# One encoder layer in fp32: operands at one place in 256 bytes, and the first head's turns and scores beside the last projection

## The chip, the cores and the metric

The kernel runs on one core of one Trainium2 chip. The metric is the device time in microseconds (us) of one execution. The engines are PE (TensorE, the matmuls), PEld (its weight loads), DVE (VectorE), ACT (ScalarE), POOL (GpSimd) and SP (SyncE). SP computes nothing here: it issues DMA transfers, one after the other, in the order of its list, and SPq is its queue.

## What is computed

One layer of a hybrid encoder runs on two sequences of 512 tokens with 1024 channels each, in fp32. Eight heads of 64 channels do a dilated window attention, 512 channels go through a gated long convolution (by FFT), both are normalized and projected together, and an MLP with squared ReLU follows.

```python
def encoder_layer(x, ...):
    xn = rmsnorm(x, mix_norm)
    proj = xn @ w_in                       # q, k, v (512 columns each), u (3 x 512)
    q = rope(rmsnorm_f32(q, q_norm)); k = rope(rmsnorm_f32(k, k_norm))
    attn = dilated_attention(q, k, v).reshape(B, S, ATTN_WIDTH)
    hy = hyena_mixer(u, hy_conv_w, hy_conv_b, hy_skip, spectra)
    mixed = jnp.concatenate([rmsnorm_f32(attn, attn_out_norm), rmsnorm_f32(hy, hy_out_norm)], axis=-1)
    h = x + mixed @ w_out
    hn = rmsnorm(h, ffn_norm)
    ff = jnp.square(jax.nn.relu(hn @ w_up))
    return h + ff @ w_down
```

The window branches of the attention are one masked softmax here: the mask and the weights of the branches lie in one table of biases (128 rows, 896 columns, `c_bias`), from which each 128 x 512 block of scores reads a shifted window.

## The kernel before

Every fp32 product is made of three matmuls on numbers split into a high and a low part (`mm3`, L85 to L92: high by high, high by low, low by high). A split costs one ACT copy, which rounds to the high part, and one DVE subtraction.

The stages, in the order of time: norm of the inputs; the projection to u (`proj_u`, psum tiles `psu`); the projection to q, k and v (`proj_qkv`, L539, `psq`, six calls, each of one of q, k, v and half of its columns, the last one Q21: v, second half); beside these the two streams of the convolution (HA and HB in the code, `psf` and `psi` are the matmuls of their FFTs, `z` is their running product, `hy_d` its copy in DRAM); then the attention with the hyena half of the output projection beside it; the attention's half of the output projection; the MLP's up projection (`pu`, `pn` from `hn`) and its down projection (`chi`, `clo`).

The attention goes by pairs of heads. `attn_load` (L778) brings q and k of a pair (tiles `qin`, two transfers each) and v. `stage_t(j, k)` (L795) turns q or k of pair j on PE with four 128 x 128 transposes into one psum bank `psk`, and splits the bank for both heads into tiles `qk`; of k it copies the high and the low part to the other 64 partitions by DMA (L812, `qk<-qk` in the trace, on SP). `stage_a(n, t)` (L815) makes a 128 x 512 block of scores of head n with two matmuls (`pss`), adds the bias and takes the maximum on DVE (`pe<-pss,bias`) and the exponential on ACT. `stage_b` (L834) turns four blocks of exponentials (`psp`) and splits the turned block into `ph`, `pl`; `stage_v` (L845) multiplies with v (`pv`). `attention` (L898) loads two pairs, turns k and q of pair 0, makes five blocks of scores ahead, and then goes through the heads.

`w_out_hyena` (L950) runs beside the attention: it loads the weights (`wur`, L758, four transfers of 512 KB), reads the convolution's result back (`hyr`, L958, two buffers), turns it (`psm`, L768) and multiplies (`psw`). It begins when both streams HA and HB are done.

`interleave` (L499) sets in which order the streams give their instructions to a scheduler, by costs that each step names; the scheduler then sets the order on every engine, and each engine runs its own list in that order. So a PE instruction that waits for a DMA holds up all PE work behind it, and a transfer in SP's list whose data isn't there holds up all transfers behind it.

Tiles lie in pools that open and close: `la` and `lw` (left side) hold the projection's inputs and weights, the raw weights `wraw`, the outputs `y`/`qo`/`vo` and the small tiles with the tag `ut`; `start_attention` (L707) closes both, opens `rm` and `lb` in their place and loads the bias table (L716). `lb` holds everything of the attention, its eight buffers of exponentials `pe` among them. The pool `cp`, opened first, stays to the end and lies below all others on the left side. In the MLP, `hn[k, half]` is in two pools: half 0 on the right side, half 1 (`hnB`) on the left.

Worked out from the allocation of the program: before, the large tiles on the left side start at byte 128 within 256 (the split inputs `xh`, `xl` and weights `whi`, `wlo` of the projections, `qk`, `bias`, `v`, `mh`, `ml`, half 1 of `hn`, among others) or at byte 32 (`pe`, `ph`, `pl`); those on the right side start at byte 224 (`chl`, `yh`, `yl`, half 0 of `hn`, `chi`, `clo`).

Of the kernel before, what the change touches and what calls it, by code (L numbers as in the profile page):

```python
# [8 lines left out]
F32 = mybir.dt.float32  # L9
F32R = mybir.dt.float32r  # L10
# [15 lines left out]
WB = 6  # L26
# [24 lines left out]
def r32(t):  # L51
    return t.bitcast(F32R)
# [3 lines left out]
def hybrid_encoder_kernel(ctx: ExitStack, tc: tile.TileContext, i: dict, outs, dbg=None):  # L56
# [62 lines left out]
    ssh = cp.tile([128, 8, 4], F32, name="ssh")  # L119
    ones = cp.tile([128, 1], F32, name="ones")  # L120
    nc.vector.memset(ones, 1.0)
    rsc = cp.tile([128, 4, 8], F32, name="rsc")
    ssd = cp.tile([128, 2, 8], F32, name="ssd")
# [8 lines left out]


    la, la_close = open_pool("la")
    lw, lw_close = open_pool("lw")
# [35 lines left out]
    def norm_x(s):  # L171
        for t in range(4):
            x = xs[s, t]
            c = slice(4 * s + t, 4 * s + t + 1)
            junk = [lw.tile([128, 512], F32, name="junk", tag=("y", "ut")[k], bufs=2) for k in range(2)]
# [20 lines left out]
    def load_w(src, first=False):  # L196

        out = []
        for k in range(src.shape[1]):
            hi = lw.tile([128, 512], F32R, name="whi", tag="whi", bufs=WB)  # L200
            lo = lw.tile([128, 512], F32R, name="wlo", tag="wlo", bufs=WB)
            raw = (re_.tile([128, 512], F32, name="wraw", tag="t", bufs=TB) if first and k > 1 else
                   lw.tile([128, 512], F32, name="wraw", tag="wraw", bufs=4))
            nc.sync.dma_start(raw, src[:, k])
            act(hi, raw)
            tt(nc.vector, lo, raw, f32(hi), ALU.subtract)
            out.append((hi, lo))
        return out
# [165 lines left out]
    def proj_u(q, w=None):  # L374
# [4 lines left out]
        def turn(s, a, y):  # L379
            pt = bank("pst", "tr", [128, 4, 128])  # L380
            for t in range(4):
                nc.tensor.transpose(pt[:, t], y[:, t * 128:(t + 1) * 128], ident)  # L382
            ut = lw.tile([128, 4, 128], F32, name="ut", tag="ut", bufs=2)
            act(ut, pt)
# [136 lines left out]
    def rope_tables():  # L521
        cs = lw.tile([128, 4, 2, 32], F32, name="cs", tag="y", bufs=2)
        nc.sync.dma_start(cs, i["c_rope"])
        g = lw.tile([128, 2, 64], F32, name="g", tag="ut", bufs=2)
# [4 lines left out]
        ng = lw.tile([128, 2, 64], F32, name="ng", tag="ut", bufs=2)  # L529
        nc.gpsimd.tensor_scalar(ng, g, -1.0, None, op0=ALU.mult)  # L530
# [8 lines left out]
    def proj_qkv(which, half):  # L539

        w = [(hi[:, c:c + 256], lo[:, c:c + 256]) for hi, lo in load_w(w_qkv[which, half]) for c in (0, 256)]
        for mp in range(4):
            s, t0 = divmod(2 * mp, 4)
# [16 lines left out]
            o = lw.tile([128, 2, 256], F32, name="qo", tag="y", bufs=2)  # L560
            sq = lw.tile([128, 2, 256], F32, name="sq", tag="ut", bufs=2)
            rr = lw.tile([128, 8], F32, name="rr", tag="rr", bufs=3)
# [19 lines left out]

    ab = lw.tile([128, 4, 4, 64], F32, name="ab")
    w0 = load_w(w_u[0], first=True)
# [193 lines left out]
    def attn_load(p, s):  # L778
        ins = []
        for src in (q_d, k_d):  # L780
            t = lb.tile([128, 4, 128], F32, name="qin", tag="qin", bufs=QIB)
            for m in range(2):
# [4 lines left out]
        nc.sync.dma_start(v2.rearrange("p t h d e -> p t (h d e)"),  # L787
                          v_d[s * S:(s + 1) * S, 2 * p:2 * p + 2].rearrange("(t p) h d e -> p t (h d e)", p=128))
        return ins[0], ins[1], r32(v2)


    PAIRS = [(s, 2 * g + p) for g in range(2) for s in range(NSEQ) for p in range(2)]
    split, ats, den_of, sta, exps, sqs = {}, {}, {}, {}, {}, {}

    def stage_t(j, k):  # L795


        ps = bank("psk", "tr")
        for t in range(4):
            lined(nc.tensor.transpose(ps[:, t * 128:(t + 1) * 128], split[j][k][:, t], ident))  # L800
        for g in range(2):
            a, b = slice(64 * g, 64 * g + 64), slice(64 - 64 * g, 128 - 64 * g)
            hi = lb.tile([128, 512], F32R, name="qk", tag="qk", bufs=QKB)
            act(hi[a], ps[a])
# [3 lines left out]
            else:  # L808
                lo = lb.tile([128, 512], F32R, name="qk", tag="qk", bufs=QKB)
                tt(nc.vector, lo[a], ps[a], f32(hi[a]), ALU.subtract)  # L810
# [4 lines left out]
    def stage_a(n, t):  # L815

        j, h = divmod(n, 2)
        if t == 0:
            if h == 0:
                den_of[j] = lb.tile([128, 4, 2], F32, name="den", tag="den", bufs=2)  # L820
            exps[n] = [lb.tile([128, 4], F32, name="mx", tag="mx", bufs=3)]
        den, mx = den_of[j], exps[n][0]
        ps = bank("pss", "ss")
        for e, kk in enumerate(sta[n, 1]):
            lined(nc.tensor.matmul(ps, lhsT=sta[n, 0][:, t * 128:(t + 1) * 128], rhs=kk, start=e == 0, stop=e == 1))  # L825
        e = lb.tile([128, 512], F32, name="pe", tag="pe", bufs=8)
        nc.vector.tensor_tensor_reduce(out=e, in0=ps, in1=bias[:, 384 - 128 * t:896 - 128 * t], scale=1.0, scalar=3e38,
                                       op0=ALU.add, op1=ALU.min, accum_out=mx[:, t:t + 1])
# [69 lines left out]
    def attention():  # L898
        load_pair(0)
        load_pair(1)  # L900
        for k in (1, 0):
            stage_t(0, k)
            yield 0.4, 0.6, 0
        ahead = [(n, t) for n in range(NI) for t in range(4)]

# [4 lines left out]

        for t in range(5):
            scores()
            yield 0.47, 1.0, 0
        stage_t(1, 1)
        yield 0.4, 0.6, 0


        for n in range(NI + 1):
# [6 lines left out]
            for t in range(4 if n < NI else 3):  # L925
# [11 lines left out]
                if t == (1, 3)[k] and j < len(PAIRS):  # L937
                    stage_t(j, k)
                    yield 0.4, 0.6, 0
                if scores():  # L940
                    yield 0.47, 1.0, 0
                if t and n < NI:
# [6 lines left out]
    def w_out_hyena():  # L949
# [4 lines left out]
        for s in range(NSEQ):  # L954
# [6 lines left out]
            for t in range(4):  # L961
# [17 lines left out]
        stream(("HA", ("r",), hyenas((0, 2)))),  # L979
        stream(("HB", ("r",), hyenas((1, 3)))),  # L980
        stream(*[(f"U{q}", (), proj_u(q, w0 if q == 0 else None)) for q in range(4)],
               *[(f"Q{w}{g}", (), proj_qkv(w, g)) for g in range(2) for w in range(3)],
               ("B", (), start_attention()), ("A", (), attention())),
        stream(("C", ("HA", "HB", "S"), w_out_hyena()), ("D", (), end_w_out_hyena()), ("E", ("A0",), w_out_first()),
# [109 lines left out]
    w_out_part(1, between)  # L1094
    rm_close.close()
    hnB, hnB_close = open_pool("hnB")
    hn_pool(hnB, 1)
# [383 lines left out]
```

## Time and profile before

| what | us |
|---|---|
| median of 3 runs (lowest, highest) | 1307.53 (1306.56, 1308.41) |
| the profiled execution, its own time | 1307.71 |
| its span, first to last instruction | 1305.9 |

| stretch, us from the span's start | what runs |
|---|---|
| 340 to 434 | q, k, v projections with the convolution streams beside them; the last projection ends near 431 |
| 434 to 481 | the end of stream HB, the first pairs of the attention, loads of the output projection |
| 481 to 640 | attention with the hyena half of the output projection beside it |
| 640 to 700 | attention's half of the output projection, norm |
| 700 to 985 | MLP up, 128 x 512 matmuls back to back |
| 1000 to 1290 | MLP down |

The page gives busy time by engine. A time between the starts of two matmuls is what one of them costs when PE is never idle, since a matmul's own duration overlaps with its successors. PEclk is the clock that was granted to PE, as a share of its full speed.

### The profile page before, as it was taken

Reading aid. Unit: us, or ns where it says so; the run is one execution under the profiler, and the core shown is the slowest. Engines: PE = TensorE matmul, PEld = TensorE weight load, DVE = VectorE, ACT = ScalarE, POOL = GpSimd, SP = SyncE. Lnnn points to the kernel's source line nnn. Section 1 sums busy time; section 2 is a strip of 40 time slices with the busy share of each in tenths; the row PEclk is TensorE's granted clock in tenths of the full one; section 3 lists DMA queues with packets and bytes.
Section 4 is the critical chain, followed back from the end, with each engine's and each line's share of the span. In section 5 each row is a group of like instructions: output and inputs, shape, how many; then the busy total and the mean of one; then the engine's idle time right before and its main releaser. Section 6 shows DMA issues by size and latency. Waiting matters only on the chain.

```text
span 1305.9 us, 18860 instructions
## 1 busy us (share of the span) xinstructions
PE 1258.5 (96%) x6733; PEld 1066.4 (82%) x6733; DVE 1013.9 (78%) x1584; ACT 650.5 (50%) x1430; POOL 175.6 (13%) x151
## 2 busy tenths in 40 slices
PE   6999999999999679999999999999999999999998
PEld 5788889999999568787777888888887888887887
DVE  6787668898997678978479877777757688578884
ACT  6444435664565485767456533343335654333350
POOL 2110002452343131124031000000000000001000
PEclk9999999999999889999999999999999999999999
DMA  7545433224411694535323544454347853473223
GB/s 244 182 138 178 148 108 101 92 90 143 138 66 66 185 269 157 153 99 185 118 92 113 173 162 142 145 161 138 129 156 279 290 160 115 161 257 93 88 70 121
DMA packets 137988, 192.82 MB, mean 148 GB/s; under 512 B 10332, under 2 KB 71684, under 8 KB 137893
## 3 DMA queue, kind: packets, MB, share of 16 engines
q1 hardware_dynamic: 136452, 185.06, 44.2%
q0 software_dynamic: 864, 4.46, 0.9%
q10 hardware_dynamic: 576, 2.10, 0.4%
q8 instruction: 53, 0.87, 0.3%
q14 instruction: 43, 0.34, 0.1%
HBM read 124.72 MB, written 62.65 MB: 143 GB/s over the span
## 4 chain that ended last, share of the span: by engine, by line
PE 79%; DVE 10%; DMA 5%; ACT 3%; issue 2%; SPq 1%; POOL 0%; DVEq 0%; ACTq 0%; POOLq 0%
PE pu L91 24%; PE pn L91 19%; PE psu L91 9%; PE psq L91 7%; PE psw L91 6%; PE psf L91 4%; PE psi L91 2%; PE pv L852 2%; PE psp L838 2%; PE pss L825 2%; DVE t L70 1%; DVE clo L70 1%; DMA qk<-qk 1%; DMA y<-h_s 1%; PE pst L382 1%
## 5 line engine op out<-in xcount | busy, mean ns | idle before, releaser
L91 PE MATMUL pu<-hn,chl 128*128 128x512 f32 x768 | 188.4, 395 | 1.8 <-POOL hn L70 1.8
L91 PEld LDWEIGHTS pu<-hn,chl 128*128 128x128 f32 x768 | 144.0, 188 | 35.7 <-POOL hn L70 2.3
L91 PE MATMUL pn<-hn,chl 128*128 128x512 f32 x576 | 143.4, 395 | 2.0 <-ACT chl L67 1.7
L91 PEld LDWEIGHTS pn<-hn,chl 128*128 128x128 f32 x576 | 108.0, 188 | 28.7 <-ACT chl L67 2.6
L67 ACT ACTIVATE chi<-fa 128x1024 fp32r<-128x1024 f32 x49 | 51.9, 1060 | 122.6 <-PE pu L91 61.7
L91 PE MATMUL psq<-whi,xh 128*128 128x256 f32 x384 | 108.7, 283 | 0.0
L91 PE MATMUL psq<-whi,xl 128*128 128x256 f32 x384 | 108.7, 283 | 0.0
L91 PE MATMUL psq<-wlo,xh 128*128 128x256 f32 x384 | 108.6, 283 | 0.0
L70 DVE TENSOR_TENSOR clo<-fa,chi 128x1024 fp32r<-128x1024 f32 x49 | 61.2, 1249 | 39.2 <-ACT chi L67 39.2
L91 PE MATMUL pu<-chi 128*128 128x512 f32 x248 | 85.1, 391 | 2.0 <-DVE chi L70 1.1
L67 ACT ACTIVATE chl<-tmp 128x512 fp32r<-128x512 f32 x64 | 40.3, 631 | 84.6 <-PE pu L91 50.4
L91 PE MATMUL pu<-clo,chi 128*128 128x512 f32 x200 | 78.3, 392 | 1.8 <-DVE clo L70 1.8
L91 PE MATMUL pn<-chi 128*128 128x512 f32 x228 | 79.2, 390 | 0.0
L91 PE MATMUL psu<-xh,whi 128*128 128x512 f32 x192 | 77.7, 408 | 0.5 <-ACT xh L67 0.5
L91 PE MATMUL pu<-chi,clo 128*128 128x512 f32 x200 | 77.9, 390 | 0.0
L91 PE MATMUL psf<-ih,dft 128*128 128x256 f32 x384 | 77.1, 283 | 0.1
L91 PE MATMUL psu<-xl,whi 128*128 128x512 f32 x192 | 76.6, 399 | 0.0
L91 PE MATMUL psu<-xh,wlo 128*128 128x512 f32 x192 | 76.1, 396 | 0.0
L91 PE MATMUL pn<-clo,chi 128*128 128x512 f32 x192 | 75.0, 391 | 0.1
L91 PE MATMUL pn<-chi,clo 128*128 128x512 f32 x192 | 74.8, 390 | 0.0
L67 ACT ACTIVATE chl<-wur 128x512 fp32r<-128x512 f32 x64 | 39.4, 629 | 70.2 <-PE pu L91 41.6
L91 PEld LDWEIGHTS psq<-whi,xh 128*128 128x128 f32 x384 | 73.4, 191 | 0.1
(245 smaller groups left out, 3211.2 us busy)
## 6 DMA issues: line engine op xcount, KB each, us to landing
fa<-f_d SPq DMA_DIRECT2D x49, 512.0 KB
wur<-in_w_up_t_dram SPq DMA_DIRECT2D x32, 512.0 KB
f_d<-x SPq DMA_DIRECT2D x60, 256.0 KB
wd<-in_w_down_dram SPq DMA_DIRECT2D x14, 1024.0 KB
f_d<-s SPq DMA_DIRECT2D x45, 256.0 KB
wraw<-in_w_u_dram SPq DMA_DIRECT2D x24, 256.0 KB
u_d<-ut SPq DMA_DIRECT2D x24, 256.0 KB
z<-u_d SPq DMA_DIRECT2D x24, 256.0 KB
```

The lines of the kernel that those rows point to most:

```text
L67: nc.scalar.activation(out, in_, func, **kw)
L70: eng.tensor_tensor(out, a, b, op=op)
L91: pin(nc.tensor.matmul(ps, lhsT=w, rhs=x, start=start and k == 0, stop=stop and k == n - 1))
L382: nc.tensor.transpose(pt[:, t], y[:, t * 128:(t + 1) * 128], ident)
L825: lined(nc.tensor.matmul(ps, lhsT=sta[n, 0][:, t * 128:(t + 1) * 128], rhs=kk, start=e == 0, stop=e == 1))
L838: lined(nc.tensor.transpose(ps[:, t * 128:(t + 1) * 128], exps[n][1 + t][:, kt * 128:(kt + 1) * 128], ident))
L852: lined(nc.tensor.matmul(pvs[n], lhsT=w, rhs=x, start=kt == 0 and e == 0, stop=kt == 3 and e == 1))
```

## The change

Two things are changed.

First, the tile `ones` in `cp` becomes 52 columns wide instead of 1, of which one is used, and the tiles `den` and `mx` of the attention move to `cp`. Worked out from the allocation, the large tiles of both sides then start at byte 224 within 256.

Second, a new pool `le` (16 KB a partition) is opened under `la` and `lw` and kept until half 1 of `hn` needs its room. The raw weights `wraw`, the tiles with tag `ut` and the tile `ab` lie in it. When the weights of the last projection have been asked for (key `W21`), a new stream X (`early`) loads a second copy of the bias table into the room of `ab`, q and k of pair 0 into rooms of `wraw`, turns them and splits them for head 0 alone into the rooms of `whi` and `wlo`, and makes the four blocks of scores and exponentials of head 0. All of it is listed beside the last projection. The attention takes the exponentials' eight buffers from `le` for all heads. At its own start it turns q and k of pair 0 a second time, now for head 1, turns k of pair 1 next, and lists the scores from head 1 on, in the first head's round two, two and one blocks at a time.

```diff
-    ones = cp.tile([128, 1], F32, name="ones")
+    ones = cp.tile([128, 52], F32, name="ones")[:, :1]
...
+    le, le_close = open_pool("le")
     la, la_close = open_pool("la")
     lw, lw_close = open_pool("lw")
...
-                   lw.tile([128, 512], F32, name="wraw", tag="wraw", bufs=4))
+                   le.tile([128, 512], F32, name="wraw", tag="wraw", bufs=4))
...
-            ut = lw.tile([128, 4, 128], F32, name="ut", tag="ut", bufs=2)
+            ut = le.tile([128, 4, 128], F32, name="ut", tag="ut", bufs=2)
...
         w = [(hi[:, c:c + 256], lo[:, c:c + 256]) for hi, lo in load_w(w_qkv[which, half]) for c in (0, 256)]
+        done.add(f"W{which}{half}")
...
-    ab = lw.tile([128, 4, 4, 64], F32, name="ab")
+    ab = le.tile([128, 4, 4, 64], F32, name="ab", tag="ab", bufs=1)
...
     def attn_load(p, s):
-        ins = []
-        for src in (q_d, k_d):
+        ins = raws[:]
+        for src in (q_d, k_d)[len(ins):]:
...
+        raws.clear()
...
-    def stage_t(j, k):
+    raws, bias0, two = [], [], []
+
+    def early():
+
+        bias0.append(le.tile([128, 896], F32, name="bias0", tag="ab", bufs=1))
+        for src in (q_d, k_d):
+            t = le.tile([128, 4, 128], F32, name="qin", tag="wraw", bufs=4)
+            for m in range(2):
+                nc.sync.dma_start(t[:, 2 * m:2 * m + 2], src[m, :, 0, :, :2].rearrange("p a h e -> p a (h e)"))
+            raws.append(t)
+        nc.sync.dma_start(bias0[0], i["c_bias"])
+        split[0] = raws
+        for k in (1, 0):
+            stage_t(0, k, (0,))
+            yield 0.4, 0.6, 3.0
+        for t in range(4):
+            stage_a(0, t)
+            yield 0.47, 1.0, 0.5
+
+    def exp_tile(i):
+
+        i %= 8
+        if i < 6:
+            tag, bufs = (("ut", 2), ("wraw", 4))[i > 1]
+            return le.tile([128, 512], F32, name="pe", tag=tag, bufs=bufs)
+        if i == 6:
+            two[:] = [le.tile([128, 2, 512], F32, name="pe", tag="ab", bufs=1)]
+        return two[0][:, i - 6]
+
+    def stage_t(j, k, heads=range(2)):
...
-        for g in range(2):
+        for g in heads:
...
-            hi = lb.tile([128, 512], F32R, name="qk", tag="qk", bufs=QKB)
+
+            def room(tag):
+                return (lw.tile([128, 512], F32R, name="qk", tag=tag, bufs=WB) if (j, g) == (0, 0) else
+                        lb.tile([128, 512], F32R, name="qk", tag="qk", bufs=QKB))
+            hi = room("whi")
...
-        ps = bank("pss", "ss")
+        ps = bank("pss", "ss" if n else "tr")
...
-        e = lb.tile([128, 512], F32, name="pe", tag="pe", bufs=8)
-        nc.vector.tensor_tensor_reduce(out=e, in0=ps, in1=bias[:, 384 - 128 * t:896 - 128 * t], scale=1.0, scalar=3e38,
+        e = exp_tile(4 * n + t)
+        nc.vector.tensor_tensor_reduce(out=e, in0=ps, in1=(bias if n else bias0[0])[:, 384 - 128 * t:896 - 128 * t], scale=1.0, scalar=3e38,
...
         for k in (1, 0):
-            stage_t(0, k)
+            stage_t(0, k, (1,))
             yield 0.4, 0.6, 0
-        ahead = [(n, t) for n in range(NI) for t in range(4)]
+        stage_t(1, 1)
+        yield 0.4, 0.6, 0
+        ahead = [(n, t) for n in range(1, NI) for t in range(4)]
...
-        for t in range(5):
-            scores()
-            yield 0.47, 1.0, 0
-        stage_t(1, 1)
-        yield 0.4, 0.6, 0
...
-                if scores():
-                    yield 0.47, 1.0, 0
+
+                for _ in range((0, 2, 2, 1)[t] if n == 0 else 1):
+                    if scores():
+                        yield 0.47, 1.0, 0
...
+        stream(("X", ("W21",), early())),
...
-               ("B", (), start_attention()), ("A", (), attention())),
+               ("B", ("X",), start_attention()), ("A", (), attention())),
```

On PE, just behind the convolution's last matmuls (`psi`), the list before was:

```order
L91 MATMUL psi<-yh,dft 128x256
L825 MATMUL pss<-qk 128x512 x10
L800 MATMUL psk<-ident,qin 128x128 x4
L838 MATMUL psp<-ident,pe 128x128 x4
L825 MATMUL pss<-qk 128x512 x2
L838 MATMUL psp<-ident,pe 128x128 x4
L800 MATMUL psk<-ident,qin 128x128 x4
L825 MATMUL pss<-qk 128x512 x2
```

At the same place PE's list with the change is:

```order
L91 MATMUL psi<-yh,dft 128x256
L875 MATMUL psp<-ident,pe 128x128 x8
L833 MATMUL psk<-ident,qin 128x128 x4
L862 MATMUL pss<-qk 128x512 x4
L889 MATMUL pv<-ph,v_5519 128x512
L889 MATMUL pv<-pl,v_5519 128x512
L875 MATMUL psp<-ident,pe 128x128 x4
L862 MATMUL pss<-qk 128x512 x4
```

The first work behind the convolution was the scores of head 0 (ten `pss`), which read the DMA copies of k; now it is the turns of head 0's exponentials, with head 1's scores behind them. Head 0's eight `pss` and eight turns stand between the matmuls of the last projection, in four places of two and two places of four. Eight turns of q and k of pair 0 more are in the list (72 `psk` in place of 64), right behind the last `psq`, and four turns of k of pair 1 among the last `psi`.

On SP, from the attention's first copies of k (`qk<-qk`) to the second load of the convolution's result (`hyr`) and somewhat behind it, the list before was:

```order
L812 DMA qk<-qk 64x512 x4
L783 DMA qin<-q_d 128x2x128
L783 DMA qin<-k_d 128x2x128 x2
L493 DMA hy_d<-z_3623 128x4x128 x2
L958 DMA hyr<-hy_d 128x4x128
L758 DMA wur<-in_w_out_dram 128x2x512 x4
L958 DMA hyr<-hy_d 128x4x128
L812 DMA qk<-qk 64x512 x2
L966 DMA hq<-in_x_prompt_dram 128x512 x2
L812 DMA qk<-qk 64x512
```

With the change it is:

```order
L849 DMA qk<-qk 64x512 x2
L787 DMA qin<-q_d 128x2x128 x2
L787 DMA qin<-k_d 128x2x128 x2
L787 DMA qin<-q_d 128x2x128
L849 DMA qk<-qk 64x512
L787 DMA qin<-q_d 128x2x128
L849 DMA qk<-qk 64x512 x3
L496 DMA hy_d<-z_3626 128x4x128 x2
L787 DMA qin<-k_d 128x2x128 x2
L994 DMA hyr<-hy_d 128x4x128
L762 DMA wur<-in_w_out_dram 128x2x512 x4
L994 DMA hyr<-hy_d 128x4x128
```

The four copies of k of pair 1 (`qk<-qk`) stood behind the four `wur` and the second `hyr`; now they and the two for head 1 of pair 0 stand ahead of the convolution's store `hy_d`. The second `hyr` stands behind the four `wur` in both.

On DVE, during the last projection (`vo` are its outputs, `sd`, `craw`, `il` and `t` belong to the convolution), the list before was:

```order
L70 TENSOR_TENSOR sd<-z_3623 128x512 x2
L70 TENSOR_TENSOR vo<-psq,vo 128x4x64
L73 SCALAR_TENSOR_TENSOR craw<-sd,z_3623 128x512 x2
L70 TENSOR_TENSOR il<-sd,ih 128x512 x2
L70 TENSOR_TENSOR vo<-psq,vo 128x4x64 x2
L70 TENSOR_TENSOR t_4581<-psf,hs 128x512
```

With the change it is:

```order
L70 TENSOR_TENSOR sd<-z_3626 128x512 x2
L70 TENSOR_TENSOR vo<-psq,vo 128x4x64
L864 ISA pe,mx<-pss,bias_5225 128x512
L864 ISA mx 128x1
L73 SCALAR_TENSOR_TENSOR craw<-sd,z_3626 128x512 x2
L70 TENSOR_TENSOR il<-sd,ih 128x512 x2
L864 ISA pe,mx<-pss,bias_5225 128x512
L864 ISA mx 128x1
L70 TENSOR_TENSOR vo<-psq,vo 128x4x64 x2
L70 TENSOR_TENSOR t_4584<-psf,hs 128x512
```

Four additions of the bias with their maxima now stand between the steps of the convolution, two of them as shown and two somewhat later, and two splits of k and q stand ahead of them. At the end of HB the steps `u`, `z` stand together, where before a `pe<-pss,bias` stood ahead of `z` and another inside.

## Rows read from the trace of the kernel before

**Rows 1.** The page: the span, and the chain that ended last by engine and line

```profile
span 1305.9 us, 18860 instructions
...
PE 79%; DVE 10%; DMA 5%; ACT 3%; issue 2%; SPq 1%; POOL 0%; DVEq 0%; ACTq 0%; POOLq 0%
```

**Rows 2.** Busy time by stretch: stretch, length, PE, PEld, DVE, ACT, POOL (count), clock, DMA

```profile
400.00:434.00 34.00, 34.00 (x284) 33.82 (x283) 27.70 (x48) 15.57 (x62) 9.07 (x8) 1.00 0.24 86
434.00:480.00 46.00, 28.46 (x140) 20.99 (x138) 30.54 (x64) 30.75 (x74) 14.36 (x12) 0.85 0.93 253
...
466.00:472.00 6.00, 4.83 (x18) 4.01 (x19) 1.76 (x5) 4.52 (x10) 3.51 (x4) 0.57 1.10 248
...
480.00:560.00 80.00, 77.69 (x423) 63.68 (x422) 69.30 (x139) 56.54 (x121) 10.90 (x10) 1.00 0.57 163
...
700.00:985.00 285.00, 285.00 (x1230) 230.93 (x1229) 221.35 (x355) 112.52 (x184) 1.04 (x2) 1.00 0.48 158
```

**Rows 3.** Waits of PE: who, for what, us in all, times, longest

```profile
PE pss L825 <- DMA qk<-qk: 8.7, 2, 4.8
```

**Rows 4.** Timeline of PE at the seam: start, us, instruction, count, idle before and releaser

```profile
431.10 0.28 PE L91 MATMUL psi<-yh,dft 128*128 128x256 f32 x1
...
447.24 4.09 PE L825 MATMUL pss<-qk 128*128 128x512 f32 x8 [3.90 <-DMA qk<-qk]
...
467.17 0.76 PE L825 MATMUL pss<-qk 128*128 128x512 f32 x1 [4.76 <-DMA qk<-qk]
467.73 1.06 PE L768 MATMUL psm<-ident,hyr 128*128 128x128 f32 x4
...
480.70 0.60 PE L838 MATMUL psp<-ident,pe 128*128 128x128 f32 x4
481.13 0.60 PE L877 MATMUL psr<-ident,db 128*128 128x128 f32 x4
481.49 0.71 PE L91 MATMUL psw<-chl,yh 128*128 128x512 f32 x2
```

**Rows 5.** The chain in order of time: start, us, what

```profile
441.01 6.09 DMA qk<-qk
...
457.29 9.75 DMA qk<-qk
```

**Rows 6.** Timeline of SP's queue at the seam: start, us, issue, count

```profile
413.78 19.88 SPq L558 DMA_DIRECT2D v_d<-vo  x7
...
451.63 0.91 SPq L493 DMA_DIRECT2D hy_d<-z  x2
...
453.19 3.54 SPq L758 DMA_DIRECT2D wur<-in_w_out_dram  x4
456.77 0.47 SPq L958 DMA_DIRECT2D hyr<-hy_d  x1
```

**Rows 7.** DVE groups from 430 to 560: line, instruction, count, busy, mean ns

```profile
L827 DVE CUSTOM_DVE_ANT_0 pe<-pss,bias 128x512 f32<-128x512 f32 x42 | 28.5, 683 | 9.7 <-PE pss L825 9.6
...
L70 DVE TENSOR_TENSOR qk<-psk,qk 64x512 fp32r<-64x512 f32 x24 | 16.5, 686 | 6.9 <-ACT qk L67 6.5
```

**Rows 8.** The page's groups of the up projection: line, matmul, count, busy, mean ns

```profile
L91 PE MATMUL pu<-hn,chl 128*128 128x512 f32 x768 | 188.4, 395 | 1.8 <-POOL hn L70 1.8
...
L91 PE MATMUL pn<-hn,chl 128*128 128x512 f32 x576 | 143.4, 395 | 2.0 <-ACT chl L67 1.7
```

**Rows 9.** Timeline of PE, two runs of six in the up projection, and the next

```profile
801.32 1.54 PE L91 MATMUL pn<-hn,chl 128*128 128x512 f32 x6
...
802.70 1.57 PE L91 MATMUL pn<-hn,chl 128*128 128x512 f32 x6
...
804.10 1.55 PE L91 MATMUL pu<-hn,chl 128*128 128x512 f32 x6
```

**Rows 10.** PE groups of the output projection from tiles at byte 128, whole span

```profile
L91 PE MATMUL psw<-chl,mh 128*128 128x512 f32 x88 | 28.4, 403 | 0.3 <-ACT raw L67 0.3
...
L91 PE MATMUL pu<-chl,ml 128*128 128x512 f32 x20 | 8.0, 402 | 0.0
```

More of the change, by code (lines that the diff above doesn't have):

```diff
@@ L174, in norm_x @@
             c = slice(4 * s + t, 4 * s + t + 1)
-            junk = [lw.tile([128, 512], F32, name="junk", tag=("y", "ut")[k], bufs=2) for k in range(2)]
+            junk = [(lw, le)[k].tile([128, 512], F32, name="junk", tag=("y", "ut")[k], bufs=2) for k in range(2)]
             lo, hi = x[:, :512], x[:, 512:]
@@ L523, in rope_tables @@
         nc.sync.dma_start(cs, i["c_rope"])
-        g = lw.tile([128, 2, 64], F32, name="g", tag="ut", bufs=2)
+        g = le.tile([128, 2, 64], F32, name="g", tag="ut", bufs=2)
         for k, n in enumerate(("q_norm", "k_norm")):
@@ L528, in rope_tables @@
         nc.gpsimd.tensor_scalar(g[:, 0], g[:, 0], -0.125, None, op0=ALU.mult)
-        ng = lw.tile([128, 2, 64], F32, name="ng", tag="ut", bufs=2)
+        ng = le.tile([128, 2, 64], F32, name="ng", tag="ut", bufs=2)
         nc.gpsimd.tensor_scalar(ng, g, -1.0, None, op0=ALU.mult)
@@ L560, in proj_qkv @@
             o = lw.tile([128, 2, 256], F32, name="qo", tag="y", bufs=2)
-            sq = lw.tile([128, 2, 256], F32, name="sq", tag="ut", bufs=2)
+            sq = le.tile([128, 2, 256], F32, name="sq", tag="ut", bufs=2)
             rr = lw.tile([128, 8], F32, name="rr", tag="rr", bufs=3)
@@ L808, in stage_t @@
             else:
-                lo = lb.tile([128, 512], F32R, name="qk", tag="qk", bufs=QKB)
+                lo = room("wlo")
                 tt(nc.vector, lo[a], ps[a], f32(hi[a]), ALU.subtract)
@@ L819, in stage_a @@
             if h == 0:
-                den_of[j] = lb.tile([128, 4, 2], F32, name="den", tag="den", bufs=2)
-            exps[n] = [lb.tile([128, 4], F32, name="mx", tag="mx", bufs=3)]
+                den_of[j] = cp.tile([128, 4, 2], F32, name="den", tag="den", bufs=2)
+            exps[n] = [cp.tile([128, 4], F32, name="mx", tag="mx", bufs=3)]
         den, mx = den_of[j], exps[n][0]
-        ps = bank("pss", "ss")
+        ps = bank("pss", "ss" if n else "tr")
         for e, kk in enumerate(sta[n, 1]):
             lined(nc.tensor.matmul(ps, lhsT=sta[n, 0][:, t * 128:(t + 1) * 128], rhs=kk, start=e == 0, stop=e == 1))
-        e = lb.tile([128, 512], F32, name="pe", tag="pe", bufs=8)
-        nc.vector.tensor_tensor_reduce(out=e, in0=ps, in1=bias[:, 384 - 128 * t:896 - 128 * t], scale=1.0, scalar=3e38,
+        e = exp_tile(4 * n + t)
+        nc.vector.tensor_tensor_reduce(out=e, in0=ps, in1=(bias if n else bias0[0])[:, 384 - 128 * t:896 - 128 * t], scale=1.0, scalar=3e38,
                                        op0=ALU.add, op1=ALU.min, accum_out=mx[:, t:t + 1])
@@ L1095, in hybrid_encoder_kernel @@
     rm_close.close()
+    le_close.close()
     hnB, hnB_close = open_pool("hnB")
```

## The prediction

> **What bounds the kernel now.** I read the page's chain first, then the table by stretch, then PE's waits, its timeline at the worst stretch, and SP's queue there. The chain that ended last is PE for 79% of the span [rows 1], so the time is PE's work plus PE's holes. From 400 to 434 us PE has no hole; from 434 to 480 it is busy 28.46 of 46 us, at a granted clock of 0.85; from 480 to 560 it is busy 77.69 of 80 again [rows 2]. [...] In that seam two waits for the DMA copies of k stand out, 8.7 us together [rows 3], at 447.24 and at 467.17 [rows 4]. The chain shows the same two transfers, 6.09 us from 441.01 and 9.75 us from 457.29 [rows 5]. The second was issued behind four 512 KB loads of `wur` and a `hyr` [rows 6].
>
> In the up projection PE has no hole, 285.00 of 285 us in 1230 matmuls, so 231.7 ns each [rows 2]. There only a cheaper matmul helps. Successive runs of six there start at 801.32, 802.70 and 804.10 [rows 9]: 1.38 us for a run on half 0 of `hn` (byte 224, as the other operand `chl`), 1.40 us for one on half 1 (byte 128).
>
> My sum is made against the profiled execution, 1307.71 us, which is 0.18 us over the median of the runs, 1307.53.
>
> **Part 1: places of the operands.** If six at byte 224 cost 1.38 us, that is 230.0 ns each; the mean of both halves is 231.7, so one at byte 128 costs 233.4, and moving it to 224 gives 3.4 ns. Starts are printed to 0.01 us, so one run alone fixes this to 1.7 ns only; the mean over 1230 carries it. Half of the 768 + 576 up matmuls [rows 8] read half 1: 672 x 3.4 ns = 2.3 us. Of the output projection's attention half, 192 matmuls read `mh` and `ml` at byte 128 against `chl` at 224 (four groups of 88, 44, 40 and 20, the first and the last in [rows 10]); at the same 3.4 ns that is 0.65 us. PE has hardly a hole in either stage, so it is all on the path: **-2.9 us**. Other pairs (`psu`, `psq`, `pss`) read two operands of one place already, before and after; nothing is expected of them. DVE and ACT are off the path in the long stages, so a change there is priced at nothing; the cover is PE's full list. Bounds: 0, if the two halves differ for another reason than the byte within 256 (they lie on two sides), and -5, if all 1536 matmuls gain a little.
>
> The two halves show 3.4 ns. [...]
>
> **Part 2: head 0 made early.** It removes from the seam the first ten `pss` that waited 3.90 us, with their bias additions and exponentials. By the lists of both kernels, PE has done 4 `pss`, 4 `pv`, 8 turns `psp` and 4 turns `psk` more by the first `psw`, besides 8 turns that are pure addition. A 512-column matmul is 0.23 us [rows 9], a turn 0.11 us (four in 0.43, 480.70 to 481.13 [rows 4]). So 8 x 0.23 + 12 x 0.109 = 3.15 us of work that stood behind the first `psw` now stands ahead of it.
>
> When does the first `psw` come? Before it was at 481.49, and what it needs are the four turns `psm` of `hyr`. The copies of k leave the way: SP issues all six before `hy_d` instead of four of them behind `wur`. What is late next is the second `hyr`, which has two buffers, so it could go early, but stands behind four `wur` still, and these behind `hy_d`, the convolution's store at 451.63 [rows 6]. What moves `hy_d`: eight early `pss` and eight turns put 8 x 0.23 + 8 x 0.109 = 2.7 us into the last projection, whose end goes from 431.1 to 433.8 [rows 4]; eight second turns, 0.87 us, stand behind it; and two `qk` splits on DVE of 686 ns [rows 7] now stand ahead of HB's last product, 1.4 us. Against these, HB's last steps `z` no longer stand behind the first `pe<-pss,bias`, which couldn't start before the scores at 447.24 [rows 4]. I let these cancel: `hy_d` near 452, the second `hyr` issued near 457. The copy of k issued half a us behind it before took 9.75 us [rows 5], so I take 467 for its landing, about where its turn was before (467.73 [rows 4]).
>
> Behind that turn the list before has 23 matmuls of 512 columns and 44 turns up to `psw`, 10.1 us, and took 481.49 - 467.73 = 13.76 us; the rest was half clock (4.83 us busy at 0.57 in 466 to 472 [rows 2]) and waits. The new list has 22 and 48, 10.3 us. With a shorter stretch at the lower clock, since PE has turns and `pv` to do up to 464 or so, and the same small waits, some 2.6 us beside it: `psw` near 480. The gain is (481.5 - 480) + 3.15 = **-4.65 us**. Bounds: none, if everything behind `hy_d` slips by 3 us or more, and -14, if the second `hyr` is no wait either (it lands by 461 or so, as a transfer of 128 KB took 6.09 us in the first wait [rows 5]), which leaves about 3 us of each of the two waits and the lower clock. After 480 PE is busy 97% [rows 2], so little of the gain is given back.
>
> **Part 3: what it puts into 400 to 434.** DVE gets four additions of the bias, 683 ns [rows 7] and a short read each, and two splits of 686 ns, 4.4 us in all, where it was busy 27.70 of 34 us; ACT gets as many steps and was busy 15.57 [rows 2]. The early `pss` stand in PE's list between `psq` and wait for copies of k that stand in SP's queue behind outputs of the projection, and DVE waits for the second bias table (448 KB) behind `hy_d` of the earlier blocks; behind them wait the `vo` outputs and HB's steps, and PE by its psum banks. SP's `v_d<-vo` stores come behind these issues, and begin at 413.78 [rows 6]; the queue waits for data there for 20 us, so the eight issues more fit. PE's cover is `psq` work, which was without a hole. **+0.7 us** for this, between 0 (the 6.3 us of DVE's free time take it) and 2.5 (half of the 4.4 us reaches PE). The wider tile `ones` and `den`, `mx` in `cp` cost nothing.
>
> The stretch moves a lot of data: 253 GB/s at a DMA share of 0.93 [rows 2]. [...]
>
> Sum: 1307.71 - 2.9 - 4.65 + 0.7 = 1300.9; against the median, 0.2 less: **1300.8 us**.
>
> **The rivals.**
> A, the queue still sets it. `wur` and `hyr` come as late as before or 2 us later (nothing in SP's list moves them ahead), and the first `psw` goes to about 483: the gain of part 2 is 3.15 - 1.5 = 1.65, and the time 1307.7 - 2.9 - 1.65 + 0.7 = 1303.9. For it speaks the share of DMA of 0.93 in 434 to 480; against it that the copies of k, which are out of the way, were the two largest waits.
> B, places don't matter to PE: the difference between the halves comes from the side they lie on or from the neighbours in the list. Then part 1 gives 0 and the time is 1303.7. For it, that the difference rests on one stage; against it, that the mean and the runs agree. [...]
> C, the whole seam closes: the second `hyr` comes in time too, the granted clock doesn't fall, part 2 gives 14 us: 1307.7 - 2.9 - 14 + 0.7, near 1291.5. For it speaks the 17.5 us of idle PE; against it the order `hyr`, four `wur`, `hyr`.
> D, slower: HB ends late. The DVE work (4.4 us), the splits ahead of HB's product (1.4), PE's insertions (3.6) and ACT's exponentials (about 4) all stand ahead of `z` and don't overlap. Then `hy_d`, on which `wur` and `hyr` hang, slips by 10 to 13 us. Each us of slip is a us of `psw`; with -2.9, -3.15 and +0.7 it is slower than before beyond 5.4 us, and by over 0.2% beyond 8; at 10 to 13 it gives 1312 to 1315, some 1313.5. Against it, that DVE has 6.3 us free and `z` no longer waits for scores.
>
> **How the numbers follow.** Forecast 0.52, A 0.16, B 0.13, C 0.11, D 0.08. The range must leave out no more than 2 in 10: D whole (0.08) and the better part of C; it goes from 1293.5 to 1305.5, which takes in A and B with their spread. A measurement of this kernel tells about 0.2% from no change, 2.6 us, so faster means under 1304.9. The forecast (1297 to 1304) and C are faster; A and B lie a us under that bound, so about two thirds of them. Faster 0.81, same 0.12, slower 0.07.
>
> **What would show it.** Part 1: in the up projection runs on both halves take 1.38 us, and the mean falls from 231.7 to about 230 ns; with B it stays. Part 2: no wait of PE for `qk<-qk` over 2 us; a wait of `psm` for `hyr` takes its place around 467; the first `psw` stands near 480, less with C, 483 or more with A and D. Part 3: PE in 400 to 436 has holes of under 1 us in all, and `hy_d` is issued near 452; with D it is issued beyond 460. The prediction is wrong if the first `psw` comes where I say and the gain is lost behind it, in the attention that is then ahead of its inputs.

## The result, and the profile after

The changed kernel takes 1296.80 us (median of 4 runs, 1295.50 to 1297.49) against 1307.26 us for the kernel before beside it (4 runs): 10.5 us less, ratio 0.992, 95% interval 0.9904 to 0.9936. A second series on another chip gave 1294.91 against 1307.37 us, ratio 0.9901 (0.9882 to 0.9921). The profiled execution took 1297.49 us.

The page of the changed kernel, span and chain by engine, to hold against [rows 1]:

```profile
span 1295.7 us, 18877 instructions
...
PE 81%; DVE 10%; ACT 3%; issue 2%; DMA 2%; SPq 0%; POOL 0%; DVEq 0%; ACTq 0%; POOLq 0%
```

DMA's share of the chain fell from 5% to 2%. Busy time by stretch of the changed kernel, in the columns of [rows 2]:

```profile
400.00:434.00 34.00, 34.00 (x280) 33.64 (x279) 30.03 (x57) 21.23 (x74) 8.84 (x9) 1.00 0.31 100
434.00:480.00 46.00, 30.21 (x170) 24.55 (x169) 30.90 (x61) 28.77 (x71) 14.33 (x12) 0.89 0.90 255
480.00:560.00 80.00, 78.69 (x429) 64.66 (x430) 70.17 (x142) 56.69 (x122) 10.88 (x10) 1.00 0.55 156
```

The stretch up to 434 took the early work without a hole in PE: DVE went from 27.70 to 30.03 us, ACT from 15.57 to 21.23. The seam from 434 to 480 still has 15.8 us of idle PE, against 17.5. PE's waits of the changed kernel:

```profile
PE psm L772 <- DMA hyr<-hy_d: 5.4, 2, 5.2
PE psi L91 <- ACT yh L67: 5.2, 2, 4.4
PE pv L889 <- DVE pl L70: 4.1, 3, 3.4
```

No wait for `qk<-qk`, which led [rows 3], is among them; the second `hyr` has come in its place. PE's timeline at the seam (to hold against [rows 4]):

```profile
434.55 1.04 PE L833 MATMUL psk<-ident,qin 128*128 128x128 f32 x8
...
444.29 0.38 PE L91 MATMUL psi<-yh,dft 128*128 128x256 f32 x1 [4.39 <-ACT yh L67]
...
454.36 0.50 PE L889 MATMUL pv<-pl,v 128*128 128x512 f32 x1 [3.42 <-DVE pl L70]
...
468.68 1.09 PE L772 MATMUL psm<-ident,hyr 128*128 128x128 f32 x4 [5.19 <-DMA hyr<-hy_d]
475.48 0.63 PE L772 MATMUL psm<-ident,hyr 128*128 128x128 f32 x4 [1.27 <-issue]
...
483.36 0.71 PE L91 MATMUL psw<-chl,yh 128*128 128x512 f32 x2
```

The first `psw` starts at 483.36, later than before (481.49), with more of the attention done ahead of it. SP's queue at the seam (to hold against [rows 6]), and the piece of the chain that goes with it:

```profile
413.80 23.06 SPq L562 DMA_DIRECT2D v_d<-vo  x8
...
453.73 0.92 SPq L496 DMA_DIRECT2D hy_d<-z  x2
...
456.03 0.61 SPq L994 DMA_DIRECT2D hyr<-hy_d  x1
456.68 2.07 SPq L762 DMA_DIRECT2D wur<-in_w_out_dram  x4
458.80 0.74 SPq L994 DMA_DIRECT2D hyr<-hy_d  x1
```

```profile
458.80 9.75 DMA hyr<-hy_d
```

In the up projection the table by stretch tells the cost of one matmul directly, since PE has no hole in it. From 760 to 960 us, first of the kernel before, then of the changed one:

```profile
760.00:960.00 200.00, 200.00 (x864) 162.03 (x863) 153.10 (x243) 77.23 (x125) 0.00 (x0) 1.00 0.44 144
```

```profile
760.00:960.00 200.00, 200.00 (x884) 165.62 (x883) 155.49 (x247) 77.36 (x125) 0.00 (x0) 1.00 0.43 141
```

864 matmuls in 200 us are 231.5 ns each, 884 are 226.2 ns. (A count takes in the one or two matmuls that the window's edges cut, so each of these means is some 0.5 ns low; their differences hardly change.) The changed kernel's timeline shows the same pace on both halves of `hn`: six on half 0, six on half 1 and the next run start 1.36 us apart, 226.7 ns a matmul:

```profile
800.30 1.52 PE L91 MATMUL pn<-hn,chl 128*128 128x512 f32 x6
...
801.66 1.52 PE L91 MATMUL pn<-hn,chl 128*128 128x512 f32 x6
...
803.02 3.33 PE L91 MATMUL pu<-hn,chl 128*128 128x512 f32 x14
```

From its first matmul to its last the up projection went from 318.4 us (669.17 to 987.56) to 312.0 (664.87 to 976.88). By the stages of the two profiled executions (starts of the first or last matmul of each), 6.4 us of the 10.2 us between them come from the up projection, and most of the rest from the stretch between the last projection and the output projection's attention half; the down projection changed by +0.55 us.

### The profile page after: what moved, and what is told of

Read it like the earlier page. It is cut to its first block, busy times and chain, and to the rows that moved or that the text cites. A ratio compares the mean times of both kernels' runs of the same rounds, so it can differ in the third digit from the quotient of the medians.

```text
span 1295.7 us, 18877 instructions
## 1 busy us (share of the span) xinstructions
PE 1251.7 (97%) x6741; PEld 1069.8 (83%) x6741; DVE 1014.0 (78%) x1584; ACT 650.6 (50%) x1430; POOL 174.0 (13%) x151
## 4 chain that ended last, share of the span: by engine, by line
PE 81%; DVE 10%; ACT 3%; issue 2%; DMA 2%; SPq 0%; POOL 0%; DVEq 0%; ACTq 0%; POOLq 0%
PE pu L91 25%; PE pn L91 19%; PE psu L91 9%; PE psq L91 7%; PE psw L91 6%; PE psf L91 4%; PE psi L91 2%; PE pv L889 2%; PE pss L862 2%; PE psp L875 2%; DVE t L70 1%; DVE clo L70 1%; DMA hyr<-hy_d 1%; PE pst L385 1%; DVE g L70 1%
## 5 line engine op out<-in xcount | busy, mean ns | idle before, releaser
L91 PE MATMUL pu<-hn,chl 128*128 128x512 f32 x768 | 184.5, 390 | 2.0 <-POOL hn L70 2.0
L67 ACT ACTIVATE chi<-fa 128x1024 fp32r<-128x1024 f32 x49 | 51.9, 1060 | 124.5 <-PE pu L91 63.1
L70 DVE TENSOR_TENSOR clo<-fa,chi 128x1024 fp32r<-128x1024 f32 x49 | 61.2, 1250 | 39.4 <-ACT chi L67 39.4
L67 ACT ACTIVATE chl<-tmp 128x512 fp32r<-128x512 f32 x64 | 40.3, 631 | 78.9 <-PE pu L91 48.3
L91 PEld LDWEIGHTS psq<-wlo,xh 128*128 128x128 f32 x384 | 73.7, 192 | 0.1
```

The lines of the kernel that those rows point to most:

```text
L67: nc.scalar.activation(out, in_, func, **kw)
L70: eng.tensor_tensor(out, a, b, op=op)
L91: pin(nc.tensor.matmul(ps, lhsT=w, rhs=x, start=start and k == 0, stop=stop and k == n - 1))
```

## The experiments

**The parts apart.** The kernel before with the places alone:

```diff
-    ones = cp.tile([128, 1], F32, name="ones")
+    ones = cp.tile([128, 52], F32, name="ones")[:, :1]
-                den_of[j] = lb.tile([128, 4, 2], F32, name="den", tag="den", bufs=2)
-            exps[n] = [lb.tile([128, 4], F32, name="mx", tag="mx", bufs=3)]
+                den_of[j] = cp.tile([128, 4, 2], F32, name="den", tag="den", bufs=2)
+            exps[n] = [cp.tile([128, 4], F32, name="mx", tag="mx", bufs=3)]
```

> The kernel before with the places of the operands alone (ones 52 columns wide, den and mx in cp; nothing early). Theory: the places are worth what the up projection shows in the trace of the changed kernel, 318.4 to 312.0 us from its first to its last matmul, 6.4 us, and little elsewhere; time 1300.5, between 1299.5 and 1301.5. Rival: part of the shorter up projection comes with the early work (another layout of the pools, other neighbours in time); then the up projection stays over 314 us and the time is 1303 or more. My own term of 2.9 us would give 1304.4.

Measured 1302.66 against 1309.96 us: -7.3, ratio 0.994 (0.9925 to 0.9954). In its profile 884 matmuls stand in the same 200 us:

```profile
760.00:960.00 200.00, 200.00 (x884) 165.62 (x883) 156.46 (x249) 78.76 (x127) 0.00 (x0) 1.00 0.44 145
```

So the shorter up projection comes from the places, not from the early work. (Its first-to-last time was 313.4 us: it lost 1.4 us on the changed kernel within the stage's first 150 matmuls, among which PE has its pauses, and nothing behind them.) The output projection's attention half went from 64.0 to 63.2 us.

The changed kernel without the places:

```diff
-    ones = cp.tile([128, 52], F32, name="ones")[:, :1]
+    ones = cp.tile([128, 28], F32, name="ones")[:, :1]
```

> The changed kernel with the large tiles of the left side back at byte 128 (ones 28 columns wide): the early work alone. Theory: the two parts add up, the seam gives what remains of 10.5 us after 6.4 to 7; time 1303.5, between 1302.5 and 1304.5, up projection back at 318.4 us. Rival: the early work alone gives the 4.65 us less 0.7 that I forecast only together with the places; then the time is 1305 or more.

Measured 1303.83 against 1309.96: -6.1, ratio 0.9946 (0.9930 to 0.9963). The up projection is back at 864 matmuls in 200 us. The two parts add to 13.4 us on a chip where no series of the full change was run; with the intervals (6.0 to 9.8 and 4.8 to 9.2 us) that agrees with the 10.5 and 12.5 us that the full change gave on two others, and with the 14.4 us that its twin with both sides at byte 128 (below) gave beside the same runs of the kernel before. Either part is worth more than I forecast for it.

**What about the place counts.** Five kernels were made of the changed one, in which only the up projection's operands (and what lies with them) stand elsewhere. Half 1 of `hn` alone back at byte 128:

```diff
     hnB, hnB_close = open_pool("hnB")
+    hnB.tile([128, 40], F32, name="pad")
```

> The changed kernel with half 1 of hn alone moved back to byte 128 (a pad of 160 bytes ahead of it in its pool). Theory: one half at another place than the weights costs both halves, since they take turns; the up projection goes back to 318 us, six matmuls to 1.38 and 1.40, time +6.4, 1303.2. Rival: each matmul pays for its own place alone; then half 0 keeps 1.36 us for six, half 1 has 1.40, the up projection takes 314.5 to 315, time +2.5 to 3.

Measured 1302.12 us (2 runs; -7.8 against before, and 6.6 us more than the next kernel below, beside the same runs), and

```profile
760.00:960.00 200.00, 200.00 (x864) 161.85 (x863) 152.32 (x243) 75.78 (x123) 0.00 (x0) 1.00 0.42 138
```

864 again, the pace of the kernel before: the whole gain of the stage hangs on this one half. Its timeline has six on half 0, six on half 1 and the next run:

```profile
800.36 1.54 PE L91 MATMUL pn<-hn,chl 128*128 128x512 f32 x6
...
801.74 1.57 PE L91 MATMUL pn<-hn,chl 128*128 128x512 f32 x6
...
803.14 1.55 PE L91 MATMUL pu<-hn,chl 128*128 128x512 f32 x6
```

Half 0, whose place wasn't touched, went from 1.36 to 1.38 us for six, half 1 to 1.40. So the rival falls: a matmul doesn't pay for its own place alone, and half 0 pays for its neighbours.

Left and right side both at byte 128 (by the allocation, a pad behind the other tiles of `pd` moves the tiles of `pd` and of all pools opened after it; a pad ahead of them, as in the kernel after this one, moves only those pools):

```diff
-    ones = cp.tile([128, 52], F32, name="ones")[:, :1]
+    ones = cp.tile([128, 28], F32, name="ones")[:, :1]
...
     hnB, hnB_close = open_pool("hnB")
+    pd.tile([128, 24], F32, name="pad")
```

> The changed kernel with the left side at byte 128 and the right side from the output projection on at byte 128 too, so that both operands of the up projection stand at 128. Theory: what counts is that both are at the same place; up projection 312 us, time 1296.8 within 1.5. Rival: byte 224 itself is the better place; then the up projection takes 315 to 318 us and the time is 1300 to 1303.

Measured 1295.54 us (2 runs, beside 1309.96), and

```profile
760.00:960.00 200.00, 200.00 (x884) 165.61 (x883) 155.44 (x247) 77.01 (x125) 0.00 (x0) 1.00 0.42 140
```

884 again, 226.2 ns each: byte 224 is nothing special; that both are at one place is what counts. Then both halves of `hn` at 128 and the weights `chl` at 224:

```diff
-    ones = cp.tile([128, 52], F32, name="ones")[:, :1]
+    ones = cp.tile([128, 28], F32, name="ones")[:, :1]
...
         pd = ctx.enter_context(tc.tile_pool(name="pd", bufs=1, side="right", **SB))
+        pd.tile([128, 24], F32, name="pad")
```

> The changed kernel with both halves of hn at byte 128 and the weights chl at 224 (the rest of the left side at 128). Theory A: a moving operand at another place than the weights costs; all runs of six take 1.40 us, the up projection 320 us or more. Theory B: it is the change of the moving operand's place from one run to the next that costs; the runs take 1.36 us, the up projection 312 to 313.5 us.

Measured 1308.22 us (one run, beside 1294.91 for the changed kernel), the up projection 321.3 us from its first matmul to its last, with

```profile
760.00:960.00 200.00, 200.00 (x856) 160.76 (x855) 151.91 (x240) 76.80 (x124) 0.00 (x0) 1.00 0.43 141
```

856 matmuls, 233.6 ns each, and runs of twelve in 2.80 and 2.82 us, so 1.40 to 1.41 us for six:

```profile
799.00 2.97 PE L91 MATMUL pn<-hn,chl 128*128 128x512 f32 x12
801.80 2.98 PE L91 MATMUL pu<-hn,chl 128*128 128x512 f32 x12
804.62 1.57 PE L91 MATMUL pn<-hn,chl 128*128 128x512 f32 x6
```

It is the moving operand against the weights (theory A), not the change from run to run. It also shows the full price, 7.4 ns a matmul. With half of the matmuls at unequal places the mean still loses 5.3, well over half of it.

Half 1 at byte 32 and at byte 96 (pads of 16 and of 32 columns, 64 and 128 bytes; the diff shows the first):

```diff
     hnB, hnB_close = open_pool("hnB")
+    hnB.tile([128, 16], F32, name="pad")
```

> The changed kernel with half 1 of hn moved to byte 32, which is 64 bytes from the weights' byte 224 when places are counted around 256 (and the same place within 64). Theory: the place within 256 counts; runs of six go to 1.38 and 1.40 us, the up projection to 318 us or more. Rival: the place within 64 counts; 1.36 us and 312 to 313.5 us as in the changed kernel.

> The changed kernel with half 1 of hn at byte 96, 128 bytes from the weights' 224. Theory (the place within 256 counts): the up projection takes 317 to 320 us again, runs of six 1.38 to 1.40 us, time 5 to 7 us over the changed kernel. Rival (the place within 128 counts, so that 96 and 224 are the same): 1.36 us, 312 to 313.5 us, time of the changed kernel.

Measured 1298.66 (one run, before 1309.43 beside it) and 1299.29 us (4 runs, before 1306.67; ratio 0.9948, 0.9923 to 0.9973). Byte 32 first, then byte 96:

```profile
760.00:960.00 200.00, 200.00 (x867) 162.41 (x866) 152.80 (x242) 76.95 (x124) 0.00 (x0) 1.00 0.42 138
```

```profile
760.00:960.00 200.00, 200.00 (x869) 162.80 (x868) 152.75 (x243) 76.95 (x124) 0.00 (x0) 1.00 0.41 138
```

Both are slower than equal places: 230.7 and 230.1 ns. So neither a distance of 64 nor one of 128 bytes is as good as none, and both cost somewhat less than one of 160 (231.5 ns, half 1 at byte 128 as above; the distance counted from the weights up to the next place of `hn`). Their times, 10.8 and 7.4 us under the kernel before beside them, are too spread for a price; the counts carry it. Places in between were not tried. So it isn't enough that places agree within 64 or within 128 bytes. That they needn't agree within 512 the changed kernel shows itself: by the allocation, half 0 and the weights stand at byte 480 within 512 and half 1 at 224, and both halves take 1.36 us.

**What sets the seam.** The profile after names the second `hyr`. Two loads of it ahead of the four `wur`:

```diff
+        early_hyr = [load_hyr(0, q) for q in range(2)]
         wo = w_out_weights(1)
...
-                t = rmh.tile([128, 4, 128], F32, name="hyr", tag="hyr", bufs=2)
-                nc.sync.dma_start(t, hy_d[s * S:(s + 1) * S, q * 128:(q + 1) * 128].rearrange("(t p) c -> p t c", p=128))
+                t = early_hyr.pop(0) if early_hyr else load_hyr(s, q)
```

> The changed kernel with the first two loads of the convolution's result (hyr) issued ahead of the four wur instead of one ahead and one behind. Theory: what sets the first hyena product is the second hyr, which lands at 468.55 because 2 MB of wur are ahead of it; ahead of them it lands near 463, the wait of 5.2 us goes, the first psw comes 2 to 4 us earlier, the time falls by 2 to 4 us against the changed kernel. Rival: the weights wur or the steps of the attention set it just as well; the wait goes to psw or to the third hyr, the time stays within 1 us.

> The changed kernel as it is, on the chip of the runs beside it, so that they have it for comparison. Both theories: 10.5 us faster than the kernel before, within 1.5.

Measured 1294.70 us (ratio 0.9897, 0.9879 to 0.9915), beside 1294.91 for the changed kernel: the same. In its profile the wait went as the theory said, but others came. First two waits of the changed kernel on the same chip, then those of the kernel with two loads ahead:

```profile
PE psm L772 <- DMA hyr<-hy_d: 4.7, 2, 4.0
PE pv L889 <- DVE pl L70: 2.7, 1, 2.7
```

```profile
PE pv L889 <- DVE pl L70: 6.3, 3, 3.0
PE psi L91 <- ACT yh L67: 4.4, 1, 4.4
PE psk L833 <- DVE qk L70: 1.3, 1, 1.3
...
PE psm L772 <- DMA hyr<-hy_d: 0.2, 1, 0.2
```

`psm` waits 0.2 us for `hyr`, and the waits for DVE's splits grew. The first `psw` came 47.3 us behind the last `psq`, against 47.75 in the changed kernel on the same chip; in the eight executions here whose lists at the seam are the changed kernel's it lies between 47.1 and 48.9, so that is no difference. Four loads ahead, in four buffers, did no better:

```diff
+        early_hyr = [load_hyr(0, q) for q in range(4)]
```

> The changed kernel with all four first loads of hyr ahead of the four wur, in four buffers. Theory of the queue: as with two ahead, and the third turn's wait (1.3 us) goes too; 3 to 5 us less than the changed kernel, unless wur now come last: they are pushed back by 0.5 MB, some 2 us at 253 GB/s, and psw waits for them; then 1 to 3 us. Rival: within 1 us of the changed kernel.

Measured 1295.42 us (0.9901, 0.9880 to 0.9922). Behind the queue ACT stood out, busy 16.41 of 18 us with two `hyr` ahead (452 to 470 of that kernel):

```profile
452.00:470.00 18.00, 13.36 (x57) 9.94 (x58) 12.98 (x30) 16.41 (x47) 9.58 (x8) 0.82 0.97 307
```

So I took the convolution's last squares off it, with the loads ahead and without:

```diff
             for s in range(NSEQ):
                 sq = rh.tile([128, 4, 128], F32, name="sqh", tag="t", bufs=TH)
+                if q == 3:
+                    tt(nc.gpsimd, sq, res[:, :, s], res[:, :, s], ALU.mult)
+                    nc.vector.tensor_reduce(out=ssh[:, 4 * s:4 * s + 4, q], in_=sq, axis=AX.X, op=ALU.add)
+                    continue
                 for a in range(4):
```

> The kernel with two hyr ahead of the wur, and besides with the squares of the convolution's last quarter (sixteen ACT instructions, 2.45 us, which stand between the convolution's end and the attention's exponentials) made on POOL and summed on DVE. Theory: behind the queue the next limit of the seam is ACT, which is busy without a gap from 452 to 469; 2.45 us less on it bring the first psw forward by 1.5 to 2.5 us, time 1.5 to 2.5 us under the changed kernel. Rival: DVE, full in the same stretch and given two sums more, or the loads of wur set it; then the time is within 1 us of the changed kernel.

> The changed kernel with the squares on POOL alone, hyr as it was (one ahead, one behind the four wur). Theory: with the second hyr still late ACT has slack; within 1 us of the changed kernel. Rival: ACT is the limit whatever the order of the loads; 1.5 to 2.5 us less.

Measured 1295.98 us with the loads ahead (ratio 0.9900, 0.9885 to 0.9915) and 1295.12 without (0.9899, 0.9880 to 0.9919), beside 1309.43 for the kernel before: by the ratios the changed kernel's time. ACT did get its slack, in the kernel with the loads ahead:

```profile
452.00:470.00 18.00, 14.97 (x66) 10.23 (x66) 14.99 (x36) 13.49 (x30) 10.54 (x9) 0.81 0.98 308
```

It fell from 16.41 to 13.49 us busy, and the first `psw` still came 48.3 us behind the last `psq`. So my second theory of the seam falls as the first did. From the last `psq` to the first `psw`, first the changed kernel (on the chip of the loads ahead), then the kernel with the loads ahead and the squares on POOL, then that with the squares on POOL alone:

```profile
432.47:480.22 47.75, 32.84 (x188) 26.61 (x186) 33.70 (x67) 31.32 (x75) 15.33 (x13) 0.89 0.96 264
433.32:481.60 48.28, 35.67 (x188) 27.59 (x186) 37.10 (x74) 28.90 (x60) 17.39 (x15) 0.86 0.99 271
433.25:485.60 52.35, 38.15 (x206) 28.98 (x205) 39.95 (x80) 32.83 (x69) 17.43 (x16) 0.90 0.96 255
```

The second kernel has 2.3 us less of idle PE than the first, but its 188 matmuls keep PE busy 2.8 us longer, at a granted clock of 0.86 instead of 0.89. So waits did go, and were paid back in slower matmuls; that the clock alone did this is not shown. In the third kernel the first `psw` comes 52.3 us behind, with 18 matmuls more ahead of it, and the time is no longer: the first `psw` is a poor mark of the seam. From the last `psq` to the first matmul of the up projection the changed kernel takes 229.2 us on that chip, and the four kernels of this section 229.7 to 230.5: none shortened it. What is left there are small waits for splits and accumulations on DVE, one of 4.4 us for the convolution's last product, which all these kernels have, and, from 452 to 470 us in the kernel with the loads ahead and the squares on POOL, a DMA share of 0.98 and a granted clock of 0.81. Which of these, if any alone, sets the first `psw`, stays open.

## Why the prediction was right, and where its steps were off

The time is in the range, 4.0 us under the forecast of 1300.8: the direction and both mechanisms held, and both terms were too small.

**Part 1 (-2.9) was under half of what it was.** Places alone gave -7.3 us. The step that failed is "six at byte 224 cost 1.38 us": I took the runs on half 0 in [rows 9] as the price without the effect, since both their operands stand at 224. They carry about half of the effect themselves, as half 0 shows when half 1 alone is moved back (1.36 to 1.38 us). The undisturbed price is 226.2 ns by the count (226.7 by the starts), not 230.0, and matmuls on both halves gain 5.3 ns on the mean, not those on one of them 3.4: for the 1144 that stand behind the stage's first 200, among which PE has its pauses, this is 6.1 us of the stage's 6.4. My bound of -5 ("if all 1536 matmuls gain a little") was also too near. The trace of before had the right number: the down projection's 128 x 512 matmuls, both operands at 224 and no other place beside them, start 0.227 us apart, as this timeline of the kernel before shows (fifteen starts in 3.40 us between these two):

```profile
1043.26 0.39 PE L91 MATMUL pu<-chi,clo 128*128 128x512 f32 x1
...
1046.66 0.39 PE L91 MATMUL pu<-chi 128*128 128x512 f32 x1
```

I had looked for a pair of places inside the stage and not for a stage without the mixture. The 0.65 us for the output projection's attention half was about right: 0.8 with places alone (in the changed kernel itself the stage went from 64.0 to 63.9 us only, against 64.6 with the early work alone). The list of pairs that the places leave as they are passed over `pv`, whose operands stood at byte 32 and byte 128 before; no gain was seen there, as the last section shows.

Rival B, that places don't matter to PE, is out: the same matmuls took 226.2 ns with their operands at one place and 233.6 ns with them at two. What in the hardware makes the difference no run here shows.

**Part 2 (-4.65) with part 3 (+0.7) was near in size and wrong in its path.** The stages behind the projections give -4.9 us in the profiled execution (last projection +2.8, up to the first `psw` -1.6, from there to the attention's half of the output projection -6.1), -5.8 on the second chip, and the early work alone -6.1 by its runs.

- The projection grew by 2.8 us, as the 2.7 us of work said, and PE had no hole there: the 0.7 us of crowding wasn't there. Rival D with it.
- HB's end was priced nearly right: `hy_d` was issued at 453.73 where I said 452. Behind the last `psq`, whose place differs by 2 us between the executions, it is 19.3 us (19.4 in the second execution, on another chip), where I had some 18. The two `qk` splits ahead of HB's last product show as the wait of 4.39 us at 444.29, against 2.72 us for its counterpart before.
- The second `hyr` was the next wait, as forecast: 468.68, I had said 467.
- "First `psw` near 480" failed: 483.36, or 49 us behind the last `psq` where I had 46 (480.22 in the second execution, but there too 47.75 us behind). The 2.6 us that I allowed beside PE's work behind `psm` were 4.4, with a wait of 1.27 for the next turn and a granted clock of 0.87 and 0.85 in the two stretches of 6 us from 464 to 476, around the wait of 5.19.
- "After 480 little of the gain is given back" failed on the other side: more was gained there. From the first `psw` to the up projection took 187.7 us before and 181.5 after; 3.15 us of this is work moved ahead and 0.65 the places, so 2.4 us are left. PE's idle time in this stretch gives 1.1 of them (3.10 us instead of 4.23; 1.31 instead of 2.31 in 480 to 560); the other 1.3 no run tells apart. That the exponentials lie further ahead is the likely reason for the fewer holes, not a shown one.

So the size of part 2 came out near by luck: the first `psw` came some 3 us later than forecast, and about as much more than forecast was gained behind it.

Rival A, that the queue sets the end of the seam: its sign was seen in the profiled execution, the first `psw` at 483, but the gain came behind it. But the queue isn't the whole of it, since with `hyr` out of the way nothing moved. Rival C, the whole seam closed, would have needed more than the copies of k and `hyr`: taking away each named wait brought the next one.

## What to carry to other kernels

A price without an effect is to be read where the effect can't be, not from the less disturbed half of the stage that has it. A pause of PE that several chains reach at about the same time isn't worth the wait that the profile names: here a wait of 4 to 5 us went with no gain at all, and then 3 us of an engine's work beside it, so what a cleared wait brings should be counted up to the next chain, not to the end of the wait. And work moved ahead counts even when the point that it was to bring forward doesn't move: with the squares alone on POOL the first `psw` came later behind the last `psq` than in the kernel before (52.3 against 50.5 us), and the kernel was as fast as the changed one.

## What the runs showed of the hardware

A 128 x 512 fp32r matmul of the up projection costs 226.2 ns when the moving operand and the weights start at the same byte within 256 (both at 224, or both at 128), and 233.6 ns when the moving operand is at 128 and the weights at 224. With half 1 of `hn` alone 64 or 128 bytes from the weights the mean was 230.7 and 230.1 ns. When runs of matmuls with equal and with unequal places (128 and 224) take turns, both are slowed (1.38 and 1.40 us for six, against 1.36). In the output projection's attention half, 192 such matmuls, equal places gave 0.8 us with places alone.

Not every matmul shows it. The 128 x 256 matmuls of the projection to q, k and v (`psq`), whose operands shared a place before and after, kept their pace: fourteen in a row start 0.12 us apart in both kernels (213.86 to 215.41 before, 214.50 to 216.06 after). The turns of 128 columns kept it too (0.44 us for four), though by the allocation their places parted: `ident` stays at byte 128 while `qin` goes from 128 to 224. And two `pv` in a row, 128 x 512 as well, whose operands went from 32 and 128 to one place, took as long as before (0.47 us). Two `pv` and four turns in the chain, first before, then after:

```profile
476.78 0.47 PE pv L852 x2
...
477.69 0.44 PE psk L800 x4
```

```profile
472.17 0.47 PE pv L889 x2
...
473.08 0.44 PE psk L833 x4
```

What sets the `pv` apart no run here shows. DVE and ACT instructions took the same time at either place (on DVE `clo<-fa,chi` 1249 and 1250 ns, on ACT `chi<-fa` 1060 and 1060 ns, with `fa` at byte 128 before and at 224 after).
